# Broadcasting row factors by masked matmuls, and updating x and h in pairs of blocks, between the sub-layers of a decoder step

## The chip, the cores and the metric

One core of one Trainium2 chip runs the whole program. The metric is the device time of one execution in microseconds (us). The engines are named as in the profile: PE (TensorE, matmuls), DVE (VectorE), ACT (ScalarE), POOL (GpSimd), SP (which issues most DMAs).

## The reference, cut to what matters

A trunk of two layers with three sub-layers each is computed for 256 prompt tokens and 8 sequences of 4 sample tokens, 288 tokens in all, with 1024 features. A sub-layer is an FFN (SwiGLU, the first and third of each layer) or a token mixer (the second: attention with RG-LRU in layer 0, HGRN2 in layer 1). Around each stands the same pair of norms:

```
def _rms_norm(x, gain):
    inv = lax.rsqrt(jnp.mean(xf * xf, axis=-1, keepdims=True) + EPS)
    return (xf * inv) * gain

def _pre(x, c, g_pre, ada_w, ada_b):
    mod = silu(c) @ ada_w + ada_b
    shift, scale, gate = split(mod, 3)
    return _rms_norm(x, g_pre) * (1 + scale) + shift, gate

def _post(x, y, gate, g_post, res_w):
    return x + res_w * (1 + gate) * _rms_norm(y, g_post)
```

So between two sub-layers, here called a joint, the kernel must: finish the mean square of y over the features, take its inverse root, add the scaled y to x, take the inverse root of the mean square of the new x, and form h = x * inv * (1 + scale) + shift, the input of the next sub-layer. The shift, scale and gate are one set for the prompt and one for each of the 8 sample sequences. There are five joints (1: after the first FFN, 2: after the first mixer, 3 and 4: after FFNs, 5: after the second mixer), and an end after the sixth sub-layer.

## The kernel before, in words

Activations are stored with features on the 128 partitions, in 8 blocks of 128 features and 288 token columns. The weights come as fp32 and are split by the program into a high part (`whi`, by ACT) and a rest (`wlo`, by DVE); every product of a weight tile with activations is three matmuls in fp32r (high by high, high by rest, rest by high). `h` is therefore also stored as a high and a rest part.

The order of instructions on PE and SP is the order of the code (a manual schedule); while the code is written out, a model of the clock (`clk`, `avail`, `until`) decides where filler matmuls are put. Fillers are the adaLN products of later sub-layers (tile `ada`, weights `aw`), and, where none is ready, `warm` matmuls of no use. The order on ACT, DVE and POOL is set by the framework's scheduler, within chains that the code ties together (`Chain`: `dv`, `da`, `dg`). When one set of adaLN products is complete, ACT copies it to SBUF (tile `asb`, in `ada_finish`), PE transposes it (tile `adaT`), and DVE adds the bias (`mod`, `modA`, `modG`).

At a joint (`out_proj`, then `pre`, lines 745 to 873 and 634 to 657) the sum of squares over features is a matmul with ones (`sums`) that leaves the 288 tokens as 4 groups of 72 columns, one group on each 32 partitions, so that the Newton step of the inverse root works on 72 columns. To bring such a factor back to all partitions as a row of 288 columns, `to_diag` copies each group to its own place of a tile `diag`, and one matmul with `hot` (ones on one partition of each 32) sums them out (`spread`: tiles `yivb` for y's factor, `xivb` for x's). The last Newton step of x's factor is done on the wide tile `rt`:

```
r = tmp("rt").rearrange("p (j t) -> p j t", j=4)
v.scalar_tensor_tensor(out=r, in0=t.unsqueeze(1).to_broadcast([128, 4, NG]), scalar=1.5, in1=diag, ...)
```

The update of x by blocks is shared by DVE and POOL (`update`: POOL multiplies 7 of 8 blocks by the copy `yivs` of the factor and adds 5 of them), and h is formed block by block by DVE and ACT (`h_scale`, `h_high`, `h_low` for the prompt, `s_scale`, `s_mult`, `s_shift`, `s_high`, `s_low` for the samples). In the next sub-layer `proj_in` starts with four output blocks at once (tiles `pj0` to `pj3`, 96 matmuls), which take h block by block as it comes.

Of the kernel before, what the change touches and what calls it, by code (L numbers as in the profile page):

```python
# [19 lines left out]
NSQ = 8  # L20
# [29 lines left out]
def tile_trunk(ctx: ExitStack, tc: tile.TileContext, I: dict, O: dict):  # L50
# [4 lines left out]
    shared = set()  # L55
    held = {"V": [], "A": [], "G": []}

    def ready(*aps):
        t = 0.0
        for ap in aps:  # L60
            t = max(t, avail.get(ap.tensor.name, 0.0) + 0.12)
        return t
# [20 lines left out]
    class Timed:  # L83
# [15 lines left out]
        def note(self, name, args, kw):  # L99
# [18 lines left out]
            else:  # L118
# [3 lines left out]
                end = place(k, r + 0.12, cost(k, name, n, ins, out, kw))  # L122
            for o in (out, kw.get("accum_out")):
                if o is not None:
                    avail[o.tensor.name] = max(end, avail.get(o.tensor.name, 0.0)) if o.tensor.name in shared else end
# [55 lines left out]
    hot = cp.tile([128, 128], F32, name="hot")  # L181
    V.memset(hot, 0.0)
    for j in range(4):
        V.memset(hot[32 * j:32 * j + 1, :], 1.0)
    diag = cp.tile([128, 4, NG], F32, name="diag")
    V.memset(diag, 0.0)
    shared.add(diag.tensor.name)
# [3 lines left out]
    V.memset(ones, 1.0)  # L191

# [159 lines left out]
    def proj_in(n, hk, done, first=None):  # L352
# [6 lines left out]
        def group(js, k):  # L359
            o = 128 * k  # L360
            until(hk[k], gap=GAP if k else GAPS[4], step=ada_half)
            for j in js:
                T.matmul(pp[j], lhsT=ws[j][0][:, o:o + 128], rhs=hk[k][:, 0, :], start=k == 0, stop=False)
                T.matmul(pp[j], lhsT=ws[j][1][:, o:o + 128], rhs=hk[k][:, 0, :], start=False, stop=False)
            if first:
                first.finish(k)
            for j in js:
                T.matmul(pp[j], lhsT=ws[j][0][:, o:o + 128], rhs=hk[k][:, 1, :], start=False, stop=k == NB - 1)

        for k in range(NB):  # L370
            if first:
                first(k)
            group(range(outer), k)
            yield
        for j in range(outer):
            done(j, pp[j])
# [144 lines left out]
    def table(f):  # L521
        act(small("tab", [128, 1]), eps, f)
# [19 lines left out]
    def sums(out, t, first, last):  # L542
        for j in range(4):
            T.matmul(out[32 * j:32 * j + 32, :], lhsT=ones[:, :32], rhs=t[:, NG * j:NG * j + NG], start=first, stop=last)

    def to_diag(u, j, e):
        q = slice(32 * j, 32 * j + 32)
        if e.key == "A":
            return e.activation(diag[q, j, :], u[q, :], AF.Copy)
        return e.tensor_copy(diag[q, j, :], u[q, :])  # L550

    def newton(u, w, v, a=None, n=1):
        t = narrow("nt")
        if n == 1:
            v.tensor_tensor(out=t, in0=w, in1=u, op=OP.mult)
        else:
            v.scalar_tensor_tensor(out=t, in0=w, scalar=n * EPS, in1=u, op0=OP.add, op1=OP.mult)
        if a:
            to_diag(u, 0, v)
            to_diag(u, 1, v)  # L560
            to_diag(u, 2, a)
            to_diag(u, 3, a)
        v.scalar_tensor_tensor(out=t, in0=t, scalar=-0.5 / n, in1=u, op0=OP.mult, op1=OP.mult)
        if a:
            r = tmp("rt").rearrange("p (j t) -> p j t", j=4)
            v.scalar_tensor_tensor(out=r, in0=t.unsqueeze(1).to_broadcast([128, 4, NG]), scalar=1.5, in1=diag,
                                   op0=OP.add, op1=OP.mult)
            return r
        v.scalar_tensor_tensor(out=u, in0=t, scalar=1.5, in1=u, op0=OP.add, op1=OP.mult)

    def spread(r, name, gap):
        until(r, gap=gap, step=ada_half)
        p = aux_ps(name)[:, :NT]
        T.matmul(p, lhsT=hot, rhs=r.rearrange("p j t -> p (j t)"), start=True, stop=True)
        return p

    def x_stats(prior=None):
# [16 lines left out]
        V.tensor_scalar(out=w, in0=p, scalar1=1.0 / D, scalar2=EPS, op0=OP.mult, op1=OP.add)  # L594

    def h_tiles():
        hk = [mp.tile([128, 2, NT], F32R, tag=f"h{b}", name=f"h{b}", bufs=1) for b in range(NB)]
        return hk, tp.tile([128, NB, NSQ, TS], F32, tag="hs", name="hs", bufs=1)
# [35 lines left out]
    def pre(i, iv, update, v, a):  # L634
        mod, mA, _ = mods[i]
        hk, hs = h_tiles()
        spans = {0: 1, 1: 1, 2: 2, 4: 2, 6: 2}
        t = {}
        for b in range(NB + 1):
            n = spans.get(b)  # L640
            if b < NB:
                for q in range(b, b + (n or 0)):
                    update(q)
                if n:
                    s_scale(b, n, mA, hs, v)
# [12 lines left out]
        return hk

    def pre_first():  # L660
        mod, mA, _ = mod_of(0)
        hk, hs = h_tiles()
# [26 lines left out]
        def finish(c):  # L689
# [11 lines left out]
            s_high(hk, c, hs, A)  # L701
            h_low(hk[c], c, t, mod, V)
            s_low(hk, c, hs, V)

        def before(k):
            if k == 0:
# [38 lines left out]
    def out_proj(i, nk, hk):  # L745
        mG = mods[i][2]
        final = i == NSUB - 1
        yg = []
# [5 lines left out]

        def done(b, p):
# [10 lines left out]

            if b < NB - 1 or final:
                prompt()
                v.tensor_tensor(out=seqs(y), in0=seqs(p), in1=seqb(mG[:, b, :]), op=OP.mult)
# [3 lines left out]
            else:  # L773
                def square():
                    a.activation(ts[2][:, :NPR], pp, AF.Square, scale=g)

                st["square"], st["prompt"] = square, prompt
                v.scalar_tensor_tensor(out=ts[1][:, :NPR], in0=pp, scalar=g, in1=x[:, b, :NPR], op0=OP.mult, op1=OP.mult)
                v.tensor_tensor(out=seqs(y), in0=seqs(p), in1=seqb(mG[:, b, :]), op=OP.mult)
                ys = y[:, NPR:]  # L780
                v.tensor_tensor(out=ts[1][:, NPR:], in0=x[:, b, NPR:], in1=ys, op=OP.mult)
                v.tensor_tensor(out=ts[2][:, NPR:], in0=ys, in1=ys, op=OP.mult)
# [6 lines left out]
        def late():  # L789
# [6 lines left out]
            if not final:  # L796
                st["x"] = aux_ps("xyms")
                for t in (acc, st[NB - 2]):
                    for q in (1, 2):
                        sums(st["x"][:, NG * (q - 1):NG * q], t[q], t is acc and q == 1, False)  # L800
# [4 lines left out]
        u = narrow("yiv")  # L805
        da.add(act(u, st["y"], AF.Abs_reciprocal_sqrt, bias=eps, scale=1.0 / D))
        if not final:
            st["square"]()
            st["prompt"]()
        if final:  # L810
            r = newton(u, st["y"], dv, da, D)
        else:
            newton(u, st["y"], dv, None, D)
            to_diag(u, 2, da)
            to_diag(u, 3, da)
        if not final:
            until(st[NB - 1][1], gap=GAPS[1], step=ada_half)
            sums(st["x"][:, 0:NG], st[NB - 1][1], False, False)
            until(st[NB - 1][2], gap=GAPS[1], step=ada_half)
            sums(st["x"][:, NG:2 * NG], st[NB - 1][2], False, True)  # L820
        ivs = tp.tile([128, NT], F32, tag="ivs", name="yivs", bufs=1)
        ivx = None
        if final:
            iv = spread(r, "yivb", GAPS[2])

        def mult(b, e):
            y = yg[b // 2][:, b % 2, :]
            e.tensor_tensor(out=y, in0=y, in1=ivs if e is dg else iv, op=OP.mult)

        def add(b, e):  # L830
            e.tensor_tensor(out=x[:, b, :], in0=x[:, b, :], in1=yg[b // 2][:, b % 2, :], op=OP.add)

        def update(b):
            if b:
                mult(b, dg)
            add(b, dv if b in (0, 2, 3) else dg)

        if final:
# [12 lines left out]
        to_diag(u, 0, dv)  # L851
        dv.scalar_tensor_tensor(out=r, in0=st["x"][:, NG:2 * NG], scalar=1.0 / D, in1=u, op0=OP.mult, op1=OP.mult)
        to_diag(u, 1, dv)
        dv.scalar_tensor_tensor(out=r, in0=st["x"][:, 0:NG], scalar=2.0 / D, in1=r, op0=OP.mult, op1=OP.add)
        dv.tensor_tensor(out=r, in0=r, in1=u, op=OP.mult)
        dv.tensor_tensor(out=r, in0=r, in1=clk["xw"], op=OP.add)
        ux = narrow("xiv")
        da.add(act(ux, r, AF.Abs_reciprocal_sqrt))
        iv = spread(diag, "yivb", GAPS[2])
        y = yg[0][:, 0, :]  # L860
# [736 lines left out]
```

## Time and profile before

| | |
|---|---|
| median of 3 runs | 1321.06 us (1319.37 to 1321.22) |
| span of the profiled execution | 1320.2 us |
| PE busy | 1273.2 us (96%) |
| PE weight loads | 1175.4 us (89%) |
| DVE busy | 803.9 us (61%) |
| ACT busy | 622.3 us (47%) |
| POOL busy | 225.3 us (17%) |
| DMA | 263.47 MB, mean 200 GB/s |

The profile gives the span of its execution, from its first to its last instruction; a device time of that same execution is not listed. The span lies 0.86 us below the median of the runs. PE is busy nearly throughout, so what a joint is worth has to be read from the time in which PE waits there, and from the clock that it was granted.

### The profile page before, as it was taken

To read this page: it belongs to the slowest core of one execution; us is meant where nothing else is said; L and a number is where in the kernel's file an instruction comes from. 1 tells how busy PE (TensorE), PEld (TensorE's weight loads), DVE (VectorE), ACT (ScalarE), POOL (GpSimd) and SP (SyncE) were. 2 spreads that over 40 slices of the span, in tenths; PEclk is the share of its full clock that TensorE was granted. 3 is DMA by queue.
4 is the path that set the end of the run, shared out by engine and by line. 5 is a ranking of instruction groups with operands and counts; after the bars stand their busy time and mean duration, and the time that the engine had idled before them with its cause. 6 is when DMAs were issued, how large, how long until landed. Compare 5 with 4: busy or idle time off the path is not lost. (4 is left out here: it accounts for less than half of the span.)

```text
span 1320.2 us, 25119 instructions
## 1 busy us (share of the span) xinstructions
PE 1273.2 (96%) x10267; PEld 1175.4 (89%) x10267; DVE 803.9 (61%) x1559; ACT 622.3 (47%) x1081; POOL 225.3 (17%) x303
## 2 busy tenths in 40 slices
PE   9999999999988999999899999989999989999995
PEld 7999999877687999999799999978788989999995
DVE  7644445688667555455754445488788777555433
ACT  5534444456654444444544444453445655444441
POOL 0000003263034000011400001153343132000011
PEclk9999999999999999999999999999999999999998
DMA  9786557466527745443675555367544452544441
GB/s 365 262 316 247 200 223 251 166 265 253 201 89 287 286 164 173 174 161 119 242 285 196 191 193 190 124 251 291 222 156 149 137 187 72 205 171 160 159 160 37
DMA packets 39556, 263.47 MB, mean 200 GB/s; under 512 B 4932, under 2 KB 5764, under 8 KB 9360
## 3 DMA queue, kind: packets, MB, share of 16 engines
q1 hardware_dynamic: 35280, 249.09, 51.6%
q0 software_dynamic: 4160, 12.77, 3.0%
q8 instruction: 81, 1.33, 0.4%
q14 instruction: 35, 0.29, 0.1%
HBM read 254.69 MB, written 7.15 MB: 198 GB/s over the span
## 5 line engine op out<-in xcount | busy, mean ns | idle before, releaser
L93 PE MATMUL pj<-h,whi 128*128 128x288 f32 x3552 | 726.0, 299 | 11.1 <-DVE h L93 8.6
L93 PEld LDWEIGHTS pj<-h,whi 128*128 128x128 f32 x3552 | 570.7, 189 | 45.9 <-issue 22.1
L93 DVE TENSOR_TENSOR wlo<-raw,whi 128x1024 fp32r<-128x1024 f32 x326 | 400.3, 1238 | 290.2 <-ACT whi L93 289.8
L93 PE MATMUL pj<-h,wlo 128*128 128x288 f32 x1776 | 519.0, 295 | 0.5 <-DVE wlo L93 0.5
L93 ACT ACTIVATE whi<-raw 128x1024 fp32r<-128x1024 f32 x326 | 340.4, 1058 | 341.4 <-PE pj L93 152.7
L93 PEld LDWEIGHTS pj<-h,wlo 128*128 128x128 f32 x1776 | 336.1, 189 | 0.7 <-DVE wlo L93 0.7
L93 PE MATMUL y<-mh,whi 128*128 128x288 f32 x1408 | 280.9, 295 | 0.0
L93 PEld LDWEIGHTS y<-mh,whi 128*128 128x128 f32 x1408 | 225.9, 188 | 2.9 <-issue 2.5
L93 PE MATMUL y<-mh,wlo 128*128 128x288 f32 x704 | 207.9, 295 | 0.0
L93 POOL TENSOR_TENSOR yss<-yss,ysq 128x288 f32<-128x288 f32 x55 | 59.5, 1082 | 789.4 <-ACT ysq L93 788.1
L93 PEld LDWEIGHTS y<-mh,wlo 128*128 128x128 f32 x704 | 132.4, 188 | 0.0
L93 DVE TENSOR_TENSOR fs<-fs,pj 128x288 f32<-128x288 f32 x88 | 39.5, 453 | 98.2 <-PE pj L93 90.9
L93 PE MATMUL ada<-aw,cT 128*32 128x512 f32 (+1 forms) x656 | 67.8, 515 | 0.0
L93 ACT ACTIVATE mh<-fs 128x288 fp32r<-128x288 f32 x88 | 37.7, 433 | 59.5 <-DVE fs L93 59.5
L93 ACT ACTIVATE fs<-pj 128x288 f32<-128x288 f32 x88 | 34.8, 400 | 37.1 <-PE pj L93 37.0
L93 ACT ACTIVATE h<-hn,mod 128x256 fp32r<-128x256 f32 x48 | 24.4, 509 | 56.1 <-DVE hn L93 56.1
L93 POOL TENSOR_TENSOR yg<-yg,yivs 128x288 f32<-128x288 f32 x38 | 34.0, 905 | 91.5 <-ACT yivs L93 91.5
L93 DVE TENSOR_TENSOR mh<-fs,mh 128x288 fp32r<-128x288 f32 x88 | 39.5, 453 | 11.2 <-ACT mh L93 11.2
L93 ACT ACT_TABLE_LOAD x27 | 34.6, 1283 | 16.2 <-PE pj L93 9.5
L93 PE MATMUL y<-o,whi 128*128 128x288 f32 x192 | 40.0, 302 | 0.5 <-DVE o L93 0.5
L93 ACT ACTIVATE ysq<-y 128x288 f32<-128x288 f32 x42 | 17.0, 404 | 44.1 <-PE y L93 44.1
L93 PEld LDWEIGHTS y<-o,whi 128*128 128x128 f32 x192 | 31.7, 193 | 1.8 <-ACT o L93 0.8
(289 smaller groups left out, 1086.9 us busy)
## 6 DMA issues: line engine op xcount, KB each, us to landing
raw<-in_wf_in SPq DMA_DIRECT2D x88, 1024.0 KB, 4.9
aw<-in_w_ada SPq DMA_DIRECT2D x64, 1024.0 KB, 5.0
raw<-in_wf_out SPq DMA_DIRECT2D x44, 1024.0 KB, 4.9
raw<-in_wo_in SPq DMA_DIRECT2D x16, 1024.0 KB, 6.9
awf<-in_w_ada SPq DMA_DIRECT2D x8, 1024.0 KB, 9.2
raw<-in_we_in SPq DMA_DIRECT2D x7, 1024.0 KB, 6.9
raw<-in_we_out SPq DMA_DIRECT2D x4, 1024.0 KB, 7.8
S<-in_s POOLq DMA_DIRECT2D x16, 256.0 KB, 7.3
```

Of the source, the lines that this page charges most:

```text
L93: r = f(*args, **kw)
```

## The change

1. `spread` takes the factor as it lies (4 groups of 72 columns) and makes the row of 288 by four matmuls of 72 columns with a mask `pick` for each group. `diag`, `hot`, `to_diag` and `rt` go; the Newton step (`refine`) ends on 72 columns. The division by 1024 is moved into the ones of `sums` (`mean1`, `mean2`).
2. The update of x is on DVE alone, reading the factor from PSUM, with blocks 0 and 1 alone and then 2 and 3, 4 and 5, 6 and 7 in pairs of 576 columns. DVE then writes x times x's factor into a tile `hv`; ACT applies scale and shift twice to the prompt columns, once into h's high part and once in place, and DVE takes the difference as h's rest. POOL applies scale and shift to the sample columns of `hv`, and ACT copies these into h.
3. `proj_in` runs the matmuls with h's rest one block behind those with its high part, and its filler is set by times of each part (`h_times`).
4. At the joint's end ACT loads the table of the next sub-layer's first function, as part of the chain `da`.

```diff
-            iv = spread(diag, "yivb", GAPS[2])
-        dv.tensor_tensor(out=y, in0=y, in1=iv, op=OP.mult)
-        r = newton(ux, r, dv, da)
-        da.activation(ivs, iv, AF.Copy)
-        ivx = spread(r, "xivb", GAPS[3])
-        hk = pre(i + 1, ivx, update, dv, da)
+        ux = root(r, da, "xiv")
+        refine(ux, r, dv)
+        iv = spread(u, "yivb", GAPS[2])
+        ivx = spread(ux, "xivb", GAPS[3])
+        hk = pre(i + 1, iv, ivx, ys, dv, da, dg)
+        da.add(table(AF.Sigmoid if i % 3 == 0 else AF.Silu))
...
+    def spread(u, name, gap):
+        until(u, gap=gap, step=ada_half)
         p = aux_ps(name)[:, :NT]
-        T.matmul(p, lhsT=hot, rhs=r.rearrange("p j t -> p (j t)"), start=True, stop=True)
+        for j in range(4):
+            T.matmul(p[:, NG * j:NG * j + NG], lhsT=pick[:, j, :], rhs=u, start=True, stop=True)
...
+        def update(b, n):
+            y, xb = ys(b, n), view(b, n, x)
+            v.tensor_tensor(out=y, in0=y, in1=wide(iv, n), op=OP.mult)
+            v.tensor_tensor(out=xb, in0=xb, in1=y, op=OP.add)
+
+        def scale(b, n):
+            t = dbl(f"hv{b}") if n > 1 else tmp(f"hv{b}").unsqueeze(1)
...
+            v.tensor_tensor(out=t if n > 1 else t[:, 0, :], in0=view(b, n, x), in1=wide(ivx, n), op=OP.mult)
+            ts = t[:, :, NPR:].rearrange("p b (s t) -> p b s t", t=TS)
+            for m, op in ((mA, OP.mult), (mod, OP.add)):
+                g.tensor_tensor(out=ts, in0=ts, in1=m[:, b:b + n, 1:9].unsqueeze(3).to_broadcast([128, n, NSQ, TS]), op=op)
+            for q in range(n):
+                c = b + q
+                p = t[:, q, :NPR]
+                a.activation(hk[c][:, 0, :NPR], p, AF.Identity, scale=mA[:, c, 0:1], bias=mod[:, c, 0:1])
+                if q == 0:
+                    a.activation(hp[b // 2][:, b % 2:b % 2 + n, 0, NPR:], t[:, :, NPR:], AF.Copy)
+                h_mark(c, 0)
+                a.activation(p, p, AF.Identity, scale=mA[:, c, 0:1], bias=mod[:, c, 0:1])
+
+        def low(b, n):
+            h = hp[b // 2][:, b % 2:b % 2 + n]
+            v.tensor_tensor(out=h[:, :, 1, :], in0=vt[b][0], in1=h[:, :, 0, :].bitcast(F32), op=OP.subtract)
```

The order of instructions moves at three places that matter here. First, ACT at joint 1, before: `h0` to `h7` are the eight blocks of h, `hn` and `hs` their sources, `asb` the finished adaLN products.

```order
L93 ACTIVATE h0_2906<-hn0_2917,mod1_2291 128x256
L93 ACTIVATE h0_2906<-hs_2914 128x32
L93 ACTIVATE h1_2907<-hn1_2926,mod1_2291 128x256
L93 ACTIVATE asb_3053<-ada11_2828 128x512
L93 ACTIVATE h1_2907<-hs_2914 128x32
L93 ACTIVATE h2_2908<-hn2_2939,mod1_2291 128x256
```

And ACT at the end of the same joint in the changed kernel, where a tile `h0` to `h3` holds two blocks and `hv` is the source of h:

```order
L94 ACTIVATE h3_2897<-hv6_2943,mod1_2294,modA1_2295 128x256
L94 ACTIVATE h3_2897<-hv6_2943 128x2x32
L94 ACTIVATE hv6_2943<-hv6_2943,mod1_2294,modA1_2295 128x256
L94 ACTIVATE h3_2897<-hv6_2943,mod1_2294,modA1_2295 128x256
L94 ACTIVATE hv6_2943<-hv6_2943,mod1_2294,modA1_2295 128x256
L94 ACT_TABLE_LOAD
L94 ACTIVATE tab_2954<-eps_130 128x1
L94 ACTIVATE asb_3016<-ada11_2820 128x512
```

The copy `asb` stood behind the first block and a half of h, and now stands behind all eight blocks and the table load. Second, ACT at joint 2 of the changed kernel, around the same kind of copy:

```order
L94 ACTIVATE h2_4458<-hv4_4493,mod2_3530,modA2_3531 128x256
L94 ACTIVATE hv4_4493<-hv4_4493,mod2_3530,modA2_3531 128x256
L94 ACTIVATE asb_4548<-ada30_3970 128x512
L94 ACTIVATE h3_4459<-hv6_4505,mod2_3530,modA2_3531 128x256
L94 ACTIVATE h3_4459<-hv6_4505 128x2x32
```

There it stands behind blocks 0 to 5; before, it stood ahead of the whole joint's blocks. Third, PE at joint 1 in the changed kernel, where the transposes `adaT` that need `asb` stand between the first eight matmuls on block 0 of h and those on block 1 (joint 2 has the same place for them):

```order
L94 MATMUL pj2_2997<-h0_2894,whi_2735 128x288
L94 MATMUL pj2_2997<-h0_2894,wlo_2736 128x288
L94 MATMUL pj3_2998<-h0_2894,whi_2763 128x288
L94 MATMUL pj3_2998<-h0_2894,wlo_2764 128x288
L94 MATMUL adaT_3026<-sm_80,asb_3016 128x18 x4
L94 MATMUL pj0_2995<-h0_2894,whi_2668 128x288
L94 MATMUL pj0_2995<-h0_2894,wlo_2669 128x288
```

Before, they stood behind the twelve matmuls on block 0, at nearly the same place. At joints 3 and 4 of the changed kernel the transposes stand elsewhere (well behind the 96 matmuls, and ahead of the first of them), and at joint 5 `asb` still stands ahead of x's root.

## Rows read from the trace of the kernel before

**Rows 1.** Joints' windows, then joint 2's head: length, PE, PEld, DVE, ACT, POOL, clock.

```profile
257.00:290.00 33.00, 28.57 (x305) 21.73 (x299) 25.97 (x71) 17.00 (x43) 19.86 (x30) 1.00 0.61 224
390.00:424.00 34.00, 29.23 (x284) 21.10 (x285) 24.16 (x71) 16.42 (x39) 15.65 (x15) 0.95 0.63 231
622.00:654.00 32.00, 27.58 (x249) 21.58 (x251) 24.86 (x69) 17.32 (x40) 16.19 (x16) 0.95 0.54 206
857.00:889.00 32.00, 28.49 (x261) 21.83 (x260) 25.76 (x73) 18.03 (x40) 19.34 (x22) 0.95 0.67 246
1081.00:1113.00 32.00, 27.04 (x206) 24.38 (x206) 24.89 (x70) 15.89 (x37) 10.51 (x12) 0.89 0.09 33
...
390.00:394.00 4.00, 2.82 (x42) 1.93 (x46) 1.66 (x5) 0.85 (x2) 0.00 (x0) 0.77 0.00 0
```

**Rows 2.** Timeline of PE at joint 1: start, length, instruction, idle before and its releaser.

```profile
261.44 0.72 PE L93 MATMUL yivb<-diag,hot 128*128 128x288 f32 x2 [0.78 <-DVE diag L93]
...
264.62 0.75 PE L93 MATMUL xivb<-rt,hot 128*128 128x288 f32 x2 [1.02 <-DVE rt L93]
...
267.34 0.40 PE L93 MATMUL pj<-h,whi 128*128 128x288 f32 x1 [0.30 <-ACT h L93]
...
270.36 0.96 PE L93 MATMUL adaT<-sm,asb 128*128 128x18 f32 x8
...
273.72 0.93 PE L93 MATMUL pj<-h,whi 128*128 128x288 f32 x5 [1.26 <-DVE h L93]
274.49 0.29 PE L93 MATMUL pj<-h,wlo 128*128 128x288 f32 x1
...
285.17 1.92 PE L93 MATMUL ada<-aw,cT 128*32 128x512 f32 x16
```

**Rows 3.** Timeline of DVE and ACT at joint 1, the factor chain.

```profile
260.48 0.23 DVE L93 SCALAR_TENSOR_TENSOR yiv<-nt,yiv 128x72 f32<-128x72 f32 x1
...
262.12 0.26 ACT L93 ACTIVATE xiv<-xv 128x72 f32<-128x72 f32 x1 [0.85 <-DVE xv L93]
...
263.49 1.07 DVE L93 SCALAR_TENSOR_TENSOR rt<-nt,diag 128x288 f32<-128x288 f32 x1
```

**Rows 4.** Tiles yg and xsq, DVE: count, then shortest, median and longest in ns.

```profile
L93 DVE TENSOR_TENSOR x<-x,yg x21: 444/1043/1066, 264.5 to 1315.4; 128x288 f32<-128x288 f32 x21
L93 DVE TENSOR_TENSOR yg<-yg,yivb x10: 440/453/455, 262.2 to 1314.5; 128x288 f32<-128x288 f32 x10
...
L93 DVE TENSOR_TENSOR xsq<-xsq x3: 750/757/760, 8.2 to 10.0; 128x576 f32<-128x576 f32 x3
```

**Rows 5.** Groups of ACT by form: busy us, mean ns of one, idle before.

```profile
L93 ACT ACTIVATE h<-hn,mod 128x256 fp32r<-128x256 f32 x48 | 24.4, 509 | 56.1 <-DVE hn L93 56.1
...
L93 ACT ACTIVATE h<-hs 128x32 fp32r<-128x32 f32 x48 | 10.6, 222 | 8.7 <-DVE hs L93 7.6
L93 ACT ACTIVATE asb<-ada 128x512 f32<-128x512 f32 x11 | 6.5, 589 | 2.3 <-PE ada L93 2.2
```

**Rows 6.** Timeline of ACT after joint 5: a table load and what follows it.

```profile
1107.30 1.28 ACT L93 ACT_TABLE_LOAD   x1 [3.44 <-PE pj L93]
1108.59 0.71 ACT L93 ACTIVATE fs<-pj 128x288 f32<-128x288 f32 x2
```

**Rows 7.** Groups of POOL by form: a two-operand step and a small copy.

```profile
L93 POOL TENSOR_TENSOR K<-K,Tn 128x128 f32<-128x128 f32 x32 | 18.9, 607 | 28.2 <-PE lv L93 11.7 <-issue 10.9 <-DVE os L93 4.0
...
L93 POOL COPY qs<-q 128x32 f32<-128x32 f32 x4 | 0.8, 238 | 4.5 <-DVE mx L93 4.5
```

**Rows 8.** Timeline of joint 5: the same copy on ACT, and a wait on PE.

```profile
1083.61 0.60 ACT L93 ACTIVATE asb<-ada 128x512 f32<-128x512 f32 x1
...
1084.80 1.09 PE L93 MATMUL yivb<-diag,hot 128*128 128x288 f32 x2 [1.06 <-ACT diag L93]
```

**Rows 9.** Windows of 2 us at joint 5, where PE's clock is low.

```profile
1088.00:1090.00 2.00, 1.80 (x6) 1.52 (x7) 1.97 (x4) 0.00 (x0) 2.00 (x3) 0.50 0.01 4
1090.00:1092.00 2.00, 2.00 (x11) 2.00 (x11) 1.97 (x7) 0.89 (x3) 1.92 (x3) 0.52 0.00 0
```

**Rows 10.** Windows: the first mixer, from its first products to its last.

```profile
290.00:386.00 96.00, 92.34 (x640) 74.52 (x633) 70.72 (x161) 61.63 (x142) 22.32 (x37) 0.96 0.56 211
```

More of the change, by code (lines that the diff above doesn't have):

```diff
@@ L55, in tile_trunk @@
     shared = set()
+    parts = {}
     held = {"V": [], "A": [], "G": []}
@@ L180, in tile_trunk @@
     G.dma_start(ident, I["ident"])
[L181 to L187, printed above, removed]
+    pick = cp.tile([128, 4, 128], F32, name="pick")
+    mean1 = cp.tile([128, 32], F32, name="mean1")
+    mean2 = cp.tile([128, 32], F32, name="mean2")
     rot = cp.tile([128, 128], F32, name="rot")
@@ L191, in tile_trunk @@
     V.memset(ones, 1.0)
+    V.memset(mean1, 1.0 / D)
+    V.memset(mean2, 2.0 / D)
+    G.memset(pick, 0.0)
+    for j in range(4):
+        G.memset(pick[32 * j:32 * j + 1, j, :], 1.0)
     def warm(n):
@@ L372, in proj_in @@
                 first(k)
-            group(range(outer), k)
+            high(k)
+            if first:
+                first.finish(k)
+                low(k)
+            elif k:
+                low(k - 1)
             yield
+        if not first:
+            low(NB - 1)
         for j in range(outer):
@@ L540, in narrow, with sums @@
         return small(name, [128, NG], tag="nr", bufs=8)
-    def sums(out, t, first, last):
+    def sums(out, t, first, last, m=None):
         for j in range(4):
[L544 to L550, printed above, removed]
@@ L552, in newton, with refine @@
-    def newton(u, w, v, a=None, n=1):
+            T.matmul(out[32 * j:32 * j + 32, :], lhsT=mean1 if m is None else m, rhs=t[:, NG * j:NG * j + NG],
+                     start=first, stop=last)
+    def refine(u, w, v, add=None):
         t = narrow("nt")
-        if n == 1:
+        if add is None:
             v.tensor_tensor(out=t, in0=w, in1=u, op=OP.mult)
         else:
-            v.scalar_tensor_tensor(out=t, in0=w, scalar=n * EPS, in1=u, op0=OP.add, op1=OP.mult)
-        if a:
[L559 to L569, printed above, removed]
@@ L571, in spread, with root @@
-    def spread(r, name, gap):
-        until(r, gap=gap, step=ada_half)
+            v.scalar_tensor_tensor(out=t, in0=w, scalar=add, in1=u, op0=OP.add, op1=OP.mult)
+        v.scalar_tensor_tensor(out=t, in0=t, scalar=-0.5, in1=u, op0=OP.mult, op1=OP.mult)
+        v.scalar_tensor_tensor(out=u, in0=t, scalar=1.5, in1=u, op0=OP.add, op1=OP.mult)
+    def root(w, a, name, **kw):
+        u = narrow(name)
+        r = act(u, w, AF.Abs_reciprocal_sqrt, **kw)
+        if a:
+            a.add(r)
+        return u
@@ L799, in late @@
                     for q in (1, 2):
[L800 removed]
+                        sums(st["x"][:, NG * (q - 1):NG * q], t[q], t is acc and q == 1, False, mean2 if q == 1 else None)
         drive(proj_out(nk, hk, done, late))
```

168 lines of the change are left out of this document (85 added, 83 removed).

## The prediction, made before the changed kernel ran

> **What bounds the kernel now.** I read the page's engine shares first: PE is busy 96% of the span, so an engine that gets faster pays only where PE waits for it or where PE's clock is low. Then I read one window for each joint [rows 1]. PE's idle time is the window's length less its busy time: 4.4 us at joint 1 (33.0 - 28.57), 4.8 at joint 2, 4.4 at 3, 3.5 at 4, 5.0 at 5. The granted clock there is 1.00, 0.95, 0.95, 0.95 and 0.89; what is missing to 1.00, times the length, is work not done: 0, 1.7, 1.6, 1.6 and 3.5 us. Idle and clock together come to about 30 us over the five joints, the most that this change can address. At joint 2 a part lies ahead of it: in 390 to 394, while the first mixer's last products and their squares are awaited, PE idles 1.2 us and the clock is 0.77. The change does not touch that part, so 3.6 us are left there, and I give joint 2 no clock back.
>
> The timeline of PE at joint 1 says which waits these are [rows 2]: 0.78 before `yivb` (for `diag`), 1.02 before `xivb` (for `rt`), then 0.30, 1.07 and 1.26 for blocks of h. The timeline of DVE and ACT under it shows the chain [rows 3]: Newton steps of 0.23 us that start 0.27 apart, x's root on ACT at 262.12, and the wide `rt` of 1.07 us.
>
> **The factors.** I work this out on joint 1's clock. y's factor is ready at 260.7 in both kernels. Removing `diag` frees two copies between the steps of `xv`, but their four links still need what they need now, and x's root stays at 262.1, ending at 262.4. Three Newton steps of 72 columns take 3 x 0.27, to 263.2, where `rt` ended at 264.56. `spread` becomes four matmuls of 72 columns. The trace has no such spread; bounds are the two fp32 passes of today, 0.75 us [rows 2], and the eight short passes of `adaT`, 0.96 [rows 2]. Eight passes is the nearer row: I take 1.0, and `xivb` is there at 264.3 instead of 265.4. PE pays 0.3 us more for each of two spreads, **+0.6 per joint**.
>
> **x and h.** DVE then multiplies, adds and scales block 0. A multiply with a PSUM operand took 440 to 455 ns, the two-SBUF add 444 at best and 1043 at the median, when POOL works beside it; 576 columns took 757 [rows 4]. So 3 x 0.45 for a block alone and 3 x 0.76 for a pair, plus `low` of 0.45 or 0.76: counting from 264.3 less one multiply and add that need only `yivb`, `hv0` is ready at 264.85, `hv2` and 3 at 269.15, `hv4` and 5 at 272.0, `hv6` and 7 at 275.15. ACT makes h's high part in 0.51 and copies the samples in 0.22 [rows 5]; POOL's two sample steps stand between. A step of two operands took 607 ns for 128 columns and a copy of 32 columns 238 [rows 7]: the sample steps of 32 to 64 columns lie between, nearer the copy, and I take 0.3 each. So h0 is complete at about 265.9, PE can start at 266.4 (it issues the second spread and fillers first), against 267.34, and its eight high-part matmuls (0.15 us each from the start of five to the next [rows 2]) are done at 267.5.
>
> The small waits on h go, but DVE needs 4.3 us from `hv0` to the first pair, so one wait before block 2 is left: PE is through with block 1 at 269.1 (eight high and four rest matmuls later), and h2 follows at 270.0 (269.15, two sample steps, the copy), 0.9 us later, less what filler covers. I leave **+0.5 per joint**, and 0.9 at joint 5, where no filler is left.
>
> **The moved copy `asb`.** This decides the sum. PE takes its instructions in order; `adaT`, which reads `asb`, stands after eight matmuls on block 0 at joints 1 and 2. ACT takes its own in order as well, and the copy `asb` (0.59 us [rows 5]) now stands behind the blocks of h. Joint 5 shows such a case in small: there `asb` of 0.60 is ahead of the copies to `diag`, and PE waits 1.06 for them [rows 8], against 0.78 at joint 1.
>
> At joint 1 ACT must first finish block 7: `hv6` at 275.15, five pieces (0.51, 0.22, 3 x 0.51) to 277.4. Then comes the table load of 1.28, the next instruction starting 1.29 after it [rows 6], a tiny instruction of 0.2, and `asb`: 279.7. PE stands from 267.5 to 279.7, **12.2 us**. Bounds: 10.5 if the last pair does not wait for `low` of the pair before, 14 if the sample steps cost 0.6 each. PE's queue behind `adaT` holds all the other matmuls of the four outputs and every filler, so nothing fills this.
>
> The Trainium skill (ScalarE: Activation LUTs, What ACT_TABLE_LOAD costs) gives 1283 ns for the load and 1380 ns more of drain for each switch. The load agrees with this trace and the drain does not, since the next instruction began 1.29 us after the load did; by the page the wait would be 13.6 and the forecast below 1.4 us higher.
>
> At joint 2 `asb` is behind blocks 0 to 5, with no load ahead of it. On the same clock: `hv4` at 272.0, five pieces to 274.3, `asb` to 274.9, a wait of **7.4 us** (bounds 5 and 9, by the same two unknowns). At joints 3 to 5 nothing of the kind stands.
>
> A wait costs clock too. At joint 5 PE idles 1.9 us and resumes at 1088.2 with 0.50, and 0.52 in the next 2 us [rows 9], which is the 1.2 GHz level; it is back at full near 1092. 3.8 us at half clock lose **1.9 us**, at each of the two waits (bounds 1.65 and 3.4).
>
> **The rest at no cost.** The table load only moves from the next sub-layer's first function; at joints 3 to 5 the last blocks' matmuls cover its 1.28 us, and it would be on the path if PE ran out of h there. `mean1` and `mean2` take a factor out of steps that stay. The end keeps POOL's part: 0, within 0.3. The order of high and low parts leaves 96 matmuls.
>
> **The sum**, in us:
> - joint 1: 12.2 + 0.5 + 0.6 + 1.9 - 4.4 = +10.8
> - joint 2: 7.4 + 0.5 + 0.6 + 1.9 - 3.6 = +6.8
> - joint 3: 0.5 + 0.6 - 4.4 - 1.6 = -4.9
> - joint 4: 0.5 + 0.6 - 3.5 - 1.6 = -4.0
> - joint 5: 0.9 + 0.6 - 5.0 - 1.7 (half its missing clock, the part after `xivb`) = -5.2
>
> That is +3.5 on the profiled span of 1320.2. The median lies 0.86 above the span, so **1324.6 us** against 1321.06.
>
> **The rivals.** 0.2%, 2.6 us, is about what a measurement here tells from no change.
>
> (a) The forecast: two long waits outweigh three better joints. 1322 to 1328; the low end has both waits at their lower bounds. Chance 0.43.
>
> (b) Faster: the first mixer takes up the wait of joint 1. From 290 to 386 PE is idle 3.7 us and the clock is 0.96, 3.8 us of work missing [rows 10], because its products wait for DVE and ACT. When PE stands at joint 1, these finish all of h and are ahead of PE afterwards, and the planner puts 18 more `ada` matmuls ahead of joint 2. If all 7.5 us come back, the sum is -4.0: 1317.1. It decides the sign from 3.5 us on, about half of it, and passes 0.2% from 6.1 on. Against it: the mixer's chains start from products that come later too. Chance 0.25.
>
> (c) Slower still: POOL's sample steps hold DVE. The add in x was 0.6 us longer at the median than alone [rows 4]. One such meeting for each of five groups at joint 1 and of four at joint 2 lengthens the waits by 3.0 and 2.4: 1330.0. Against it: POOL has 10 small steps per joint where it had 12 of 288 columns. Chance 0.14.
>
> The Trainium skill (SBUF — State Buffer, SBUF: two separate sides) says that a DVE instruction with two SBUF inputs and a POOL instruction reading SBUF exclude each other for a whole instruction. This trace agrees: 1043 ns against 444 for two SBUF operands, while those with a PSUM operand kept to 455.
>
> (d) No net change: the waits come out near their lower bounds (10.5 and 5, which gives 1320.5), and joints 3 to 5 give what I say. 1319 to 1322. Chance 0.18.
>
> **How the numbers follow.** Faster by over 0.2% (below 1318.4): 0.19 of (b), where most of the 7.5 us comes back, and 0.02 of (d), **0.21**. Within 0.2%: 0.06 of (b), 0.16 of (d), 0.09 of (a)'s low end, **0.31**. Slower (above 1323.7): 0.34 of (a) and 0.14 of (c), **0.48**. The range must reach from (b), with 2.1 us below it for waits that are also near their lower bounds, to (c), with 2 above it, about what the clock loss at its upper bound adds: **1315 to 1332**; the forecast alone has 1322 to 1328.
>
> **What would show it.** In the profile after, PE should wait about 12 us at joint 1 and 7 at joint 2 before `adaT`, released by ACT `asb`, with a clock near 0.5 behind each; `xivb` should come 1 us earlier after the root; waits for h at joints 3 to 5 should add up to 1 us or so; the add in x should be near 444 and 760 ns rather than 1043. I am wrong if the two waits sum to less than 15 us, if the first mixer between 290 and 386 gets shorter by several us, or if joints 3 to 5 keep over half of their idle time.

## The result and the profile after

The changed kernel takes 1342.35 us (median of 4, 1340.84 to 1343.02) where the kernel before took 1320.21 (4 runs, the three above and one more): a ratio of 1.0168, 95% interval 1.0153 to 1.0182. It is slower, as forecast, but by 22 us and not by 3.5; 1342 lies outside the range of 1315 to 1332. The profiled execution has a span of 1340.0 us against 1320.2.

The waits of PE, grouped, in the profile after (total us, times, longest):

```profile
PE adaT L94 <- ACT asb L94: 23.3, 4, 13.5
PE pv L94 <- ACT pTs L94: 8.3, 1, 8.3
PE lv L94 <- DVE Q L94: 3.1, 4, 2.4
PE rgr L94 <- DVE xc L94: 2.7, 1, 2.7
PE vtp L94 <- ACT vs L94: 2.6, 2, 1.9
PE pj L94 <- ACT h L94: 1.8, 3, 1.3
```

The first row is the forecast wait. The second was not forecast at all: `pv` belongs to the attention of the first mixer, about 110 us behind joint 1. Waits for h have shrunk to 1.8 us in the whole program (11.1 before). The windows of the five joints, which answer to [rows 1] (length, then busy PE, PEld, DVE, ACT, POOL, clock):

```profile
256.50:289.50 33.00, 19.38 (x223) 15.45 (x212) 15.62 (x35) 15.86 (x34) 16.09 (x33) 0.74 0.70 237
414.00:448.00 34.00, 25.55 (x260) 20.22 (x259) 18.21 (x40) 18.32 (x38) 9.71 (x14) 0.85 0.55 209
652.00:684.00 32.00, 29.83 (x303) 23.46 (x302) 22.16 (x43) 21.13 (x43) 9.32 (x13) 1.00 0.65 246
880.00:912.00 32.00, 31.83 (x316) 24.97 (x316) 22.40 (x45) 21.73 (x44) 14.13 (x21) 1.00 0.78 285
1104.00:1136.00 32.00, 28.57 (x237) 26.38 (x237) 22.37 (x45) 20.04 (x41) 4.48 (x10) 1.00 0.23 81
```

Joints 3 to 5 are better, at full clock, but not as good as forecast: they idle 2.2, 0.2 and 3.4 us (4.4, 3.5 and 5.0 before), where the sum left 0.5, 0.5 and 0.9. At joint 3, 1.5 us of it is a filler `ada` that waits for its weights; at joint 5, 1.2 us stand ahead of `xivb` and 1.3 are for h. Joints 1 and 2 idle 13.6 and 8.5 us, at 0.74 and 0.85.

To see where 19.8 us of span come from I cut both profiles at the start of y's root on ACT (`yiv`, one for each sub-layer) and, in the first mixer, at the first `rgr` matmul on PE:

| stretch | before | after | measured | of it `ada` | forecast |
|---|---|---|---|---|---|
| start to joint 1 | 259.5 | 259.0 | -0.5 | 0 | 0 |
| joint 1 to the first `rgr` | 33.1 | 46.2 | +13.1 | +1.2 | +10.8 |
| first `rgr` to joint 2 | 101.7 | 112.7 | **+11.0** | +4.9 | 0 |
| joint 2 to joint 3 | 229.2 | 235.3 | +6.2 | -1.4 | +6.8 |
| joint 3 to joint 4 | 234.9 | 227.7 | -7.2 | -3.0 | -4.9 |
| joint 4 to joint 5 | 224.1 | 224.1 | **0** | -0.6 | -4.0 |
| joint 5 to the end's root | 224.4 | 221.7 | -2.7 | 0 | -5.2 |
| the end | 13.4 | 13.3 | -0.2 | 0 | 0 |

The column `ada` is the change in PE's busy time on the filler products. In all of the program it is only 1.1 us, but the planner has moved fillers from the later stretches into the first mixer. The windows from the first `rgr` to joint 2, before and after, for all of PE and other engines and then for `ada` on PE alone:

```profile
292.54:394.21 101.67, 94.71 (x702) 76.12 (x704) 73.65 (x166) 65.27 (x151) 24.34 (x37) 0.96 0.51 194
305.19:417.91 112.72, 99.82 (x746) 76.06 (x744) 75.69 (x165) 65.72 (x151) 26.24 (x37) 0.94 0.56 210
...
292.54:394.21 101.67, 8.63 (x68) 0.96 0.51 194
305.19:417.91 112.72, 13.56 (x104) 0.94 0.56 210
```

So of the +11.0 us, 4.9 are work that the later stretches are spared, and 5.9 are idle time (7.0 to 12.9): the loss of the first mixer is about 6 us. A stretch of a single execution is good to about 3 us only: experiments 10 and 11 below run the same code up to joint 4, and their stretches from joint 1 to joint 2 are 132.3 and 135.5 us, at clocks of 0.98 and 0.96.

Joint 1 in the timelines of PE, of ACT and of POOL, which answer to [rows 2, 3] and show the chain of the forecast wait:

```profile
260.23 1.11 PE L94 MATMUL yivb<-yiv,pick 128*128 128x72 f32 x8
262.70 1.11 PE L94 MATMUL xivb<-xiv,pick 128*128 128x72 f32 x8
265.63 0.40 PE L94 MATMUL pj<-h,whi 128*128 128x288 f32 x1
...
280.48 1.89 PE L94 MATMUL adaT<-sm,asb 128*128 128x18 f32 x8 [13.52 <-ACT asb L94]
```

```profile
276.56 0.26 ACT L94 ACTIVATE h<-hv 128x64 fp32r<-128x64 f32 x1 [1.09 <-POOL hv L94]
...
278.44 1.28 ACT L94 ACT_TABLE_LOAD   x1
279.74 0.20 ACT L94 ACTIVATE tab<-eps 128x1 f32<-128x1 f32 x1
279.85 0.58 ACT L94 ACTIVATE asb<-ada 128x512 f32<-128x512 f32 x1
```

```profile
274.92 0.75 POOL L94 TENSOR_TENSOR hv<-hv,modA 128x64 f32<-128x64 f32 x1 [1.47 <-DVE hv L94]
275.61 0.58 POOL L1005 DMA_DIRECT2D msk<-in_msk  x1
276.21 0.31 POOL L94 TENSOR_TENSOR hv<-hv,mod 128x64 f32<-128x64 f32 x1
```

PE spreads x's factor 3.7 us after the root (5.2 before), reaches block 0 at 265.6 and stands from 267.0 to 280.5. ACT goes through eight blocks, the table load and `tab`; `tab` starts 1.30 us after the load, so the drain behind a switch that the Trainium skill adds (ScalarE: Activation LUTs, What ACT_TABLE_LOAD costs) is not in this trace either. What the third fence shows is new: POOL issues a load of the next mixer (`msk`) between the two sample steps of the last pair, and ACT waits 1.09 us for them. That, and pieces of 0.59 us on ACT for 0.51, make the 13.5 us out of the forecast 12.2.

The clock behind the wait, in windows of 2 us:

```profile
280.00:282.00 2.00, 1.52 (x8) 1.52 (x8) 0.00 (x0) 2.00 (x4) 1.32 (x2) 0.50 0.82 229
282.00:284.00 2.00, 2.00 (x9) 2.00 (x10) 0.47 (x2) 0.71 (x2) 0.86 (x2) 0.50 0.80 289
284.00:286.00 2.00, 2.00 (x18) 1.49 (x21) 0.00 (x0) 0.00 (x0) 1.98 (x4) 0.60 1.04 361
```

From 286 on it is 1.00.

And ACT in the first mixer, ahead of the unforeseen wait, with PE's row behind it:

```profile
365.96 1.28 ACT L94 ACT_TABLE_LOAD   x1
367.25 1.26 ACT L94 ACTIVATE gx<-gx 128x576 f32<-128x576 f32 x2
368.53 1.28 ACT L94 ACT_TABLE_LOAD   x1
...
369.93 1.43 ACT L94 ACTIVATE m<-ob 128x288 fp32r<-128x288 f32 x4
371.26 0.58 ACT L94 ACTIVATE pTs<-pT 128x512 f32<-128x512 f32 x1
```

```profile
362.96 0.66 PE L94 MATMUL pT<-ident,sm 128*128 128x128 f32 x4
371.89 1.97 PE L94 MATMUL pv<-pTs,vt 128*64 128x512 f32 x2 [8.27 <-ACT pTs L94]
```

PE has made the transposes `pT` by 363.6. ACT copies them (`pTs`) only behind the sample softmax, two table loads, the gelu `gx` and four copies `m`. In the kernel before, the fifth of the six copies `pTs` stood ahead of all of this and the sixth behind the first gelu, as ACT's timeline of before shows. The change does not touch the mixer's code.

```profile
344.57 0.60 ACT L93 ACTIVATE pTs<-pT 128x512 f32<-128x512 f32 x1 [1.78 <-PE pT L93]
...
347.99 1.28 ACT L93 ACT_TABLE_LOAD   x1
349.28 0.68 ACT L93 ACTIVATE gx<-gx 128x576 f32<-128x576 f32 x1
...
350.03 0.59 ACT L93 ACTIVATE pTs<-pT 128x512 f32<-128x512 f32 x1
```

### The profile page after: what moved, and what is told of

It is laid out like the page before. It is cut to its first block, busy times and chain, and to the rows that moved or that the text cites. A ratio compares the mean times of both kernels' runs of the same rounds, so it can differ in the third digit from the quotient of the medians.

```text
span 1340.0 us, 25184 instructions
## 1 busy us (share of the span) xinstructions
PE 1277.4 (95%) x10381; PEld 1182.8 (88%) x10381; DVE 781.6 (58%) x1411; ACT 636.9 (48%) x1087; POOL 198.3 (15%) x298
## 4 chain that ended last, share of the span: by engine, by line
PE 83%; DVE 7%; ACT 4%; issue 2%; DMA 1%; POOL 1%; SPq 0%; DVEq 0%; POOLq 0%; ACTq 0%
PE pj L94 48%; PE y L94 24%; PE ada L94 3%; DVE wlo L94 1%; PE lv L94 1%; POOL hv L94 1%; PE adaT L94 1%; ACT hv L94 1%; DVE x L94 1%; ACT whi L94 1%; DVE hv L94 1%; ACT L94 1%; PE o L94 1%; DVE yg L94 1%; ACT h L94 1%
## 5 line engine op out<-in xcount | busy, mean ns | idle before, releaser
L94 PE MATMUL ada<-aw,cT 128*32 128x256 f32 (+1 forms) x696 | 68.9, 500 | 1.5 <-DMA aw<-in_w_ada 1.5
L94 ACT ACTIVATE fs<-pj 128x288 f32<-128x288 f32 x88 | 34.7, 399 | 38.9 <-PE pj L94 38.9
L94 PEld LDWEIGHTS ada<-aw,cT 128*32 128x32 f32 x696 | 17.3, 111 | 21.6 <-issue 15.2
L94 ACT ACTIVATE h<-hv,mod,modA 128x256 fp32r<-128x256 f32 x40 | 23.7, 592 | 21.0 <-DVE hv L94 21.0
L94 DVE TENSOR_TENSOR yg<-y,modG 128x32 f32<-128x32 f32 x48 | 8.9, 186 | 40.6 <-ACT yg L94 40.6
```

What stands on the lines that cost most here:

```text
L94: r = f(*args, **kw)
```

## The experiments

**Theory**: the time is lost where PE, in order, meets an instruction that another in-order engine reaches late. There are three such places: `adaT` behind `asb`; POOL's queue at joint 1; and the first mixer, whose order has changed though its code has not. **Rivals**: the pace of the new update on DVE and POOL is itself too slow; or the mixer is late only because joint 1 is.

**1. The changed kernel, `adaT` held back** behind the 96 matmuls.

```diff
-        yield [asb]
+        yield max(clk.get("joint", -99.0) + 20.0 - clk["t"], 0.5)
```

> The changed kernel with the transposes adaT held back to 20 us of the planner's clock behind each joint, so that they stand behind the 96 matmuls of joints 1 and 2; the order that results on ACT in the first mixer has the six copies pTs ahead of the gelu and its two table loads again. Theory (the time is PE's own standing time behind asb at joints 1 and 2 and behind pTs in the first mixer, plus low clock after each): waits of 13.5, 7.6 and 8.3 us go, and about 2.4 us of clock after each of the first two and 4.6 after the third; 1342 - 38 = 1304 us, within 5. Rival 1 (the joints' own pace on DVE and POOL is what is slow): the waits turn into waits for h, and it stays above 1325. Rival 2 (the mixer's wait follows from the late start of joint 1 and not from ACT's order): the same 1304, and only the next two runs tell it apart.

Measured: 1330.51 us, ratio 1.0084 (1.0063 to 1.0105). The waits for `asb` at the joints and for `pTs` went, as expected, but only 12 us came back and not 38: a miss, above the 1325 of the first rival. But the pace of the update is not what PE waits for. A wait that had been hidden stands in the place of the first, as PE's and POOL's timelines show:

```profile
295.88 0.71 PE L94 MATMUL xms<-xsq,mean 128*32 128x72 f32 x16 [11.14 <-POOL xsq L94]
```

```profile
278.52 1.07 POOL L1006 DMA_DIRECT2D rgw<-in_rgw  x2
285.15 0.77 POOL L1028 DMA_DIRECT2D out_k_old<-kc  x1 [5.56 <-DMA kc<-in_kc]
...
289.98 1.41 POOL L94 TENSOR_TENSOR xsq<-xsq 128x576 f32<-128x576 f32 x1
```

POOL holds the store `out_k_old` until the load of `kc` has landed, and the adds of `xsq` (and the first parts of the mixer's `xr`) stand behind it. In the kernel before, five of the eight loads were issued some 50 us ahead of joint 1, and the last three with one store shortly before it (POOL's timeline of before):

```profile
249.45 0.56 POOL L970 DMA_DIRECT2D vc<-in_vc  x1 [6.89 <-PE y L93]
250.00 1.07 POOL L970 DMA_DIRECT2D rgw<-in_rgw  x2
252.71 0.55 POOL L993 DMA_DIRECT2D out_v_old<-vc  x1 [1.64 <-DMA vc<-in_vc]
```

The pair tiles `hv` come from the same ring of buffers as the mixer's tiles, and are taken first.

**2 and 3. The changed kernel, sample attention after the prompt part**; alone, and with `adaT` held back.

```diff
-            side(att_prompt(0, 0, aux_ps("pv0"), True))
-            yield EV
-            side(att_sample())
+            side(att_prompt(0, 0, aux_ps("pv0"), True, att_sample))
```

> The changed kernel with the sample part of the first mixer's attention started when its last prompt part is through, so that all copies pTs stand ahead of the gelu on ACT; joint 1 is as in the changed kernel, and asb at joint 2 happens to come ahead of the blocks. Theory (the wait for pTs comes from ACT's order in the mixer): joint 1 keeps its 13.5 us, pv loses its 8.3 and the clock 4.6, joint 2 loses 7.6 and 2.3: 1342 - 23 = 1319 us, within 5. Rival 2 (that wait follows from the wait at joint 1, whatever the order): only joint 2's 10 us go, and pv or the next products wait about 8 us as before: 1332 us.

> The changed kernel with both edits, adaT held back and the attention's sample part after the prompt part. Theory: as with adaT held back alone, 1304 us, within 5, since there the mixer's order has already come right; no more than 2 us between the two. Rival 1 (pace of the joints): above 1325.

Measured: 1340.89 us (1.0161, 1.0143 to 1.0179) and 1340.35 (1.0148, 1.0124 to 1.0173). Both miss. In the first, the wait for `pTs` fell from 8.3 to 1.6 us and the one at joint 2 went, but `pvs` then waited 4.3 for ACT, and joint 1 to joint 2 took 160.0 us (158.9 without the edit). In the second, an `adaT` of the mixer waited 8.5 for `asb`, and `xms` 9.1 for POOL as in experiment 1. In both, tying one order by hand moved the wait to another meeting.

**4. The kernel before, one instruction moved**: `asb` of joint 1 behind the eight blocks of h.

```diff
-        A.activation(asb, acc, AF.Copy)
+        r = A.activation(asb, acc, AF.Copy)
+        if (i, g) == (1, 1):
+            after(r, clk["prior"][0])
```

> The kernel before with one instruction moved: asb of joint 1 stands on ACT behind the eight blocks of h; every other instruction of every engine keeps its place. PE reaches adaT at 270.4 on the clock of before and asb would end at 279.9: a wait of about 9.4 us; one later wait of 1.3 goes, and 2.4 us of clock are lost behind it. Theory (such a wait stays to the end, and leaves the mixer behind it alone): 1320 + 10.5 = 1331 us, within 2. Rival b of the prediction (the first mixer takes the wait up): 1321 to 1326. Rival 2 (a late start upsets the mixer and adds a second wait there): 1337 or more.

Measured: 1329.04 us, 1.0067 (1.0047 to 1.0086). PE waits 9.33 us there:

```profile
280.48 1.89 PE L93 MATMUL adaT<-sm,asb 128*128 128x18 f32 x8 [9.33 <-ACT asb L93]
```

The table shows what the mixer does behind it, in us after y's root at joint 1 (first `rgr`, first scores `sc`, first sample products `pvs`):

| kernel | `rgr` | `sc` | `pvs` | `rgr` to `sc` | `sc` to `pvs` |
|---|---|---|---|---|---|
| before | 33.1 | 59.7 | 95.7 | 26.6 | 36.0 |
| before, `asb` late (4) | 44.6 | 69.9 | 105.8 | 25.3 | 35.9 |
| changed | 46.2 | 76.5 | 124.6 | 30.3 | 48.1 |
| changed, `adaT` held back (1) | 45.2 | 71.7 | 108.7 | 26.5 | 37.0 |
| loads first, `adaT` held back (6) | 34.7 | 61.2 | 103.0 | 26.5 | 41.8 |
| factors alone (8) | 31.6 | 58.6 | 94.5 | 27.0 | 35.9 |
| before, planner's clock set back (9) | 33.6 | 66.4 | 113.2 | 32.8 | 46.8 |

With the mixer's order untouched, a joint that is 11.5 us late does not lengthen the mixer: the rival that the late start upsets it falls. Rival (b) of the prediction does not fall altogether. From the first `rgr` to joint 2 PE took 97.2 us here and 101.7 before:

```profile
304.70:401.93 97.23, 92.34 (x706) 74.30 (x708) 72.35 (x163) 65.29 (x150) 24.30 (x37) 0.98 0.53 200
```

Of the 4.4 us, 2.1 are idle time (4.9 for 7.0); the clock was 0.98 for 0.96. This is one execution, the fastest of the four. In the median 9.6 us of the 11.5 are still there at the end.

**5 to 7. The changed kernel, the first mixer's buffers and loads taken ahead of `hv`**; alone, with `adaT` held back, and with both mixers' loads first.

```diff
     def pre(i, iv, ivx, ys, v, a, g):
         mod, mA, _ = mods[i]
+        if i == 1:
+            early[1] = even_loads()
         hp, hk = h_tiles()
```

> The changed kernel with one move: the buffers and loads of the first mixer (cs, msk, kc, vc, rgw) are taken in the code ahead of the joint's hv tiles, so that their DMAs stand on POOL among the last products of y, as before, and not between the sample steps and ahead of the adds of xsq. On ACT this puts asb of joint 1 behind six blocks instead of eight and the table load; the mixer's order (gelu ahead of two copies pTs) and joint 2 stay. Theory (the hv tiles push the loads into POOL's queue at joint 1, and POOL stands there for about 10 us, mostly under PE's wait for asb): the wait at joint 1 falls from 13.5 to about 8, the one for xc from 2.7 to 1.2; 1342 - 7 = 1335 us, within 3. Rival (the loads' place does nothing, PE waits for asb alone): the wait falls by what ACT's order gives, but xms or xc takes over, and it stays above 1339.

> The changed kernel with the loads first and adaT held back behind the 96 matmuls. With adaT held back alone, PE waited 11.1 us for xsq on POOL in the place of asb. Theory (both the copy asb and POOL's loads hold PE at joint 1, one under the other): with both gone no wait above 2 us is left at joint 1, and 11 us and some 3 of clock come back: 1330 - 14 = 1316 us, within 4. Rival (a third thing follows, PE meets DVE or ACT in the first mixer in any case): 1325 or more.

> As loads first with adaT held back, and the second mixer's loads (lmask, sel) taken ahead of the hv tiles of joint 4 as well. Theory (the second mixer gives joint 4's gain back through its own order, not through these two small loads): within 2 us of the kernel without it. Rival (the same push of loads costs joint 4's 4 us): 3 to 5 us less.

Measured: 1336.46 us (1.0138, 1.0112 to 1.0164), 1323.37 (1.0027, 1.0016 to 1.0039) and 1323.37 (1.0031, 1.0019 to 1.0044). The loads' place is worth 4 us by the ratios (6 by the medians) beside the late `asb`, where the two ratios are known to 2 and 3 us, and 7 without it; the second mixer's two loads are worth nothing. In the first, joint 1's wait for `asb` fell to 8.6, because the copy stood behind six blocks there, and `rgr` still waited 2.7, so that sign of POOL's queue was misread. The second is a miss: joint 1 is fast (`rgr` at 34.7), but 5.8 us are lost from `sc` to `pvs`, and it takes 1323 and not 1316.

**8. The kernel before, factors by masked matmuls alone**; POOL's share of the update and `asb` stay.

```diff
-        T.matmul(p, lhsT=hot, rhs=r.rearrange("p j t -> p (j t)"), start=True, stop=True)
+        for j in range(4):
+            T.matmul(p[:, NG * j:NG * j + NG], lhsT=pick[:, j, :], rhs=r, start=True, stop=True)
```

> The kernel before with the first part of the change alone: factors spread by four masked matmuls of 72 columns, no diag, Newton's last step on 72 columns; the update of x and h, POOL's share and the order of asb stay. The prediction's prices (xivb about 1.1 us earlier, 0.6 us more on PE): about 0.5 us less per joint, 1317.5 us, within 1.5. Rival (the whole chain ahead of h counts, with the clock that joint 5 loses): 1313 or less. Rival (PE's extra passes eat it): 1320.

Measured: 1314.18 us, **0.996 (0.994 to 0.998)**: faster than both kernels, and by more than my prices gave. In windows that stand as far from y's root as those of [rows 1], the five joints idle 2.3, 4.0, 1.8, 2.3 and 4.0 us, at clocks of 1.00, 0.95, 1.00, 1.00 and 0.95; joint 1:

```profile
257.00:290.00 33.00, 30.74 (x323) 23.56 (x313) 25.96 (x71) 16.07 (x39) 20.25 (x31) 1.00 0.61 227
```

**9. The kernel before, the planner's clock set back by 1.5 us once**, after joint 1's code.

```diff
         hk = pre(i + 1, ivx, update, dv, da)
+        if i == 0:
+            clk["t"] += -1.5
```

> The kernel before with nothing changed but the planner's idea of the time: its clock is set back by 1.5 us once, at the end of joint 1. Every operation stays; what moves is the order on PE and ACT after joint 1, and in the first mixer it comes out as in the changed kernel (gelu and its table loads ahead of two copies pTs, 18 more ada matmuls ahead of joint 2). Theory (the first mixer of the changed kernel is long because of this order, not because of joint 1's wait or of the new update): from the first scores to the first pvs it takes 48 us as there, and not 36; 1320 + 12 to 16 = 1332 to 1336 us. Rival (the order costs nothing when joint 1 is undisturbed, since PE's waits there come from the late start): within 3 us of 1320.

Measured: 1333.85 us, 1.0107 (1.0087 to 1.0127). No operation of the reference differs; the order does (and some `warm` matmuls, 1.6 us of them up to joint 2). ACT and PE show the changed kernel's mixer:

```profile
357.10 1.28 ACT L93 ACT_TABLE_LOAD   x1
358.39 1.26 ACT L93 ACTIVATE gx<-gx 128x576 f32<-128x576 f32 x2
359.67 1.28 ACT L93 ACT_TABLE_LOAD   x1
...
362.40 0.57 ACT L93 ACTIVATE pTs<-pT 128x512 f32<-128x512 f32 x1
```

```profile
363.03 1.97 PE L93 MATMUL pv<-pTs,vt 128*64 128x512 f32 x2 [6.90 <-ACT pTs L93]
```

Joint 1 to joint 2 takes 150.2 us here, 15.4 more than before, but not on the same work: 6.0 us of it are fillers `ada` (the stretches behind joint 2 have 5.0 less), 1.6 are `warm`, and 6.4 are idle time. `ada` on PE in this stretch (16.1 us before):

```profile
260.13:410.28 150.15, 22.04 (x196) 0.95 0.57 219
```

From the first `rgr` to joint 2, PE idles 6.6 us more than before, where it was 5.9 in the changed kernel. So the order alone, with the old update and an undisturbed joint 1, costs the first mixer what it lost in the changed kernel. It is not the whole of the 13 us that the run lost: the second mixer's stretch, joint 4 to joint 5, idles 4.6 us more as well.

**10 and 11. The changed kernel with the old update at joints 1 and 4, ahead of the mixers; and at joint 1 alone.**

```diff
+        if i + 1 in (1, 4):
+            hk = pre_old(i + 1, iv, ivx, ys, dv, da, dg)
+        else:
             hk = pre(i + 1, iv, ivx, ys, dv, da, dg)
```

> The changed kernel with the update of x and h as before (POOL's share and all) at joints 1 and 4, which stand ahead of the mixers, and as changed at 2, 3 and 5, ahead of the FFNs; factors by masked matmuls everywhere. The first mixer's order comes out as in the kernel before, and asb stands ahead of the blocks or behind the 96 matmuls at all joints. Theory (the new update is worth something where nothing but FFN matmuls follow, and its loss is all in the joints and mixers): below the factors alone, 1314 - 3 (joints 2 and 3) - 1.5 (joint 5) = 1310 us, within 3. Rival (the new update is worth nothing by itself): 1314. Rival (the FFN joints' new order upsets the fillers later): 1318 or more.

> As with the old update at joints 1 and 4, but with the changed one at joint 4 too, ahead of the second mixer. Theory (at joint 4 the new update's gain is given back in the second mixer, whose PE order is set by DVE's chain): the stretch from joint 4 to joint 5 is 2 to 4 us longer than with the old update there, 1312 to 1314 us in all. Rival (the update of joint 4 is a gain as at the FFN joints): 1 to 2 us less than with the old one.

Measured: 1318.78 us (0.9987, 0.9971 to 1.0002) and 1328.3 (1.0053, 1.0034 to 1.0072). The first misses: joint 1 to 2 took 132.3 us and joints 2 to 4 together 1.5 less than with the factors alone (within the 3 us above), but joint 4 to 5 took 226.9 against 221.5, with 5.4 us of waits for `vs` on ACT. Its time lies where the expectation put the rival of upset fillers, but what is long is the second mixer's stretch, behind a joint 4 with the old update. Why it is long was not tried. The second misses upward, by the mechanism of joint 1 at joint 4, where the changed kernel did not have it, so it does not tell what it was to tell of the second mixer:

```profile
872.87 1.89 PE L94 MATMUL adaT<-sm,asb 128*128 128x18 f32 x8 [7.66 <-ACT asb L94]
```

**12. The changed kernel, loads first, `adaT` held back, the planner's clock set forward by 2 us at joint 1**, which gives ACT's order in the first mixer as before (the step of experiment 9, with +2 for -1.5).

> The changed kernel with its loads first and adaT held back, and the planner's clock set forward by 2 us once at the end of joint 1, which gives the first mixer the order on ACT that it has in the kernel before. Theory (three things made the changed kernel slow, adaT behind the late asb, POOL's loads in the joint, and the order in the first mixer; the new update itself is no loss): with all three gone the first mixer takes 36 to 37 us from the first scores to the first pvs, where the same without the clock's step took 42, and the stretch from joint 1 to joint 2 falls from 138 to about 133; 1323.4 - 5 = 1318.5 us, within 2.5. Rival (the new update has a loss of its own, which the order hid): 1322 or more. Rival (it is worth more than the factors alone): 1313 or less.

Measured: 1325.23 us, 1.0047 (1.0033 to 1.0061), a miss. `sc` to `pvs` fell to 38.2, but `rgr` to `sc` rose from 26.5 to 31.2, with 3.6 us of waits for `xc`; joint 1 to joint 2 stayed at 138.5. The time is where the rival of a loss of the update itself was put, which it does not prove, since the order is again another.

## Why the prediction was right in sign and wrong in size

- **The factors** (1.0 us a spread, 0.3 more on PE, `xivb` there 1.1 earlier): 1.11 us, 0.36 more; counted from the root `xivb` starts 1.5 earlier and is there 1.1 earlier, as forecast. Alone they give 5 us (experiment 8), where the expectation made 2.5 of these prices. The idle time of the five windows falls from 22.1 us [rows 1] to 14.3, by 7.8, and ten spreads at 0.36 more give 3.6 of it back; the clock at joints 3 to 5 rose as well. How the 5 us divide between the two is not shown.
- **x and h**: `hv6` and 7 were ready 15.8 us after the root, forecast 15.7. ACT's pieces took 0.59, not 0.51 (the row of [rows 5] had no scale operand). The tile view and the group of ACT in the profile after:

```profile
L94 DVE TENSOR_TENSOR x<-x,yg x31: 450/757/1059, 262.9 to 1335.1; 128x288 f32<-128x288 f32 x16, 128x576 f32<-128x576 f32 x15
```

```profile
L94 ACT ACTIVATE h<-hv,mod,modA 128x256 fp32r<-128x256 f32 x40 | 23.7, 592 | 21.0 <-DVE hv L94 21.0
```

  The add in x took 450 ns at best, and 757 at the median, which is a pair's time; before, the median was the stretched 1043 [rows 4]. The three of over 1 us here are at the end, where POOL still has its part. So rival (c) did not come.
- **`asb`**: 13.5 us for 12.2, and 7.6 for 7.4. That 13.5 lies beside the 13.6 that the prediction worked out with a drain is chance: the trace has no drain. Experiment 4 shows that such a wait stays for the most part to the end (9.3 us of it, with the low clock behind it, made 9.6).
- **The clock**: 2.6 us lost behind the first wait (0.8 from 280.5 on, then 1.0 and 0.8 in the next two windows) for 1.9.
- **Joint 1 to the first `rgr`, and joint 2 to joint 3**, came out at +13.1 and +6.2 for +10.8 and +6.8. The 2.3 us more at joint 1 are made up by the longer wait (1.3), the clock (0.7) and fillers brought forward (1.2). Beneath the wait of joint 1 lay another, POOL's queue, which the prediction missed: I counted POOL's sample steps and not the mixer's DMAs that the new tiles moved into its queue. With the loads out of that queue the kernel takes 4 to 6 us less (experiment 5, where joint 1's wait for `asb` is 4.9 shorter and would account for it), and with `adaT` held back 7 less (6 against 1).
- **The step that failed** is that the mixers stay as they are. The sum has no term for them, and rival (b) gave the first one a gain. Its stretch became 11.0 us longer: 4.9 of fillers brought forward, which rival (b) had counted as a gain and which do come back later, and 5.9 of idle time, a loss. Experiment 9 shows that the order that the planner and the scheduler make there, from a clock 1.5 us off, is enough: 6.6 us more idle time in the same stretch, and 13 us in the whole run. The order was there to be read: gelu and two table loads ahead of two copies `pTs`, which PE waits for. I had read the orders of the joints alone.
- **Joint 4** gave nothing back for the 3.3 us of idle and 1.6 of clock that it saved, though its stretch has 0.6 us fewer fillers. So the second mixer too did not stay as it was; it idles more (4.9 us against 1.7 in the 60 us that begin 72 us after the joint's window does, with waits of 3.0 us for `Q` and 1.9 for `vs`). That this is its order, as in the first mixer, is argued and not shown; its two small loads are not it (experiment 7).
- **Joints 3 and 5** together gave 9.9 us, forecast 10.1, and that is luck: 3.0 of joint 3's 7.2 are fillers that had been done ahead of joint 2. Without them the two gave 6.9 (4.2 for 4.9, and 2.7 for 5.2). The waits of joints 3 and 5 shrank less than the sum had them.

What stays open: whether the new update has a loss of its own ahead of a mixer. With all three places mended (experiment 12) the kernel is still 0.5% slower than before by its median. Its profiled execution, the fastest of the six, has the span of the one before (1320.1 us): joint 1 to joint 2 is 3.7 us longer and joint 3 to joint 4 is 3.8 shorter. Both are near what single executions differ by, so where the 0.5% are lost is not shown.

## What to carry to other kernels

Where PE's order is written by a clock model, a faster joint is also a changed clock: read the new order on every engine as far as the next stage that is not bound by PE, and look for instructions that stand ahead of one that PE waits for. Every tile taken from a shared ring, and every DMA that waits for such a buffer, moves with the edit; on an engine that also computes, a store that waits for a load holds all behind it. Take the parts apart before judging: here the factors alone are a gain, which the rest buried. Before a longer stretch is called a loss, count what filler work moved into it.

## What the runs showed of the hardware that was not expected

An ACT pass of 256 columns took 592 ns with a scale from SBUF beside the bias, and 509 with the bias alone [rows 5]. POOL took 0.54 to 0.77 us for the issue of one DMA, and up to 5.6 us where it held one back for another's landing. Waits hide under each other: taking the 13.5 us away from PE gave 12 back, with two others (7.6 and 8.3) gone as well.
